# Where low halves lie in memory, and three other edits, in a fused two-block transformer kernel

## The chip, the cores and the metric

The kernel runs on one core of a Trainium2 chip. The metric is the device time of one execution in microseconds (us). Three runs before the change took 733.15 to 735.66, median 735.49.

## The reference

One sequence of 256 tokens, width 1024, passes two blocks. All inputs and outputs are fp32.

```
mod = silu(c) @ w_ada + b_ada                  # six rows: sh1 sc1 g1 sh2 sc2 g2
h = rms(x) * (1 + sc1) + sh1
z = h @ w_in                                   # q, k, v of three mixers, 3072 gate columns
merged = sum over 3 mixers of sigmoid(zg) * (attention @ w_branch)
x = x + g1 * rms(merged @ w_out)
h = rms(x) * (1 + sc2) + sh2
a, g = split(h @ w_up)
x = x + g2 * rms((gelu(conv3(a)) * g) @ w_down)
# second block, two layers
y = gated_linear_attention(x)                  # q, k, v, g, decay; out projection
x = layer_norm(1.414 * x + y)
y = dilated_window_attention(x)                # 3 groups, 8 heads, shared k and v
x = layer_norm(1.414 * x + y)
```

## The kernel before

Every large product is done in three passes of TensorE's fp32r type: a matrix is split into a high half (`hi`, the value rounded to fp32r) and a low half (`lo`, the rest), and `mm3` (L267) adds lo x hi, hi x lo and hi x hi in PSUM. Matmuls are recorded on L262, or on L193 where a `Queue` records them.

Weights come from `Stream` (L105): chunks of 128x2048 land in three `raw` buffers through SP's queue, ScalarE makes `whi` (L158) and VectorE `wlo` (L159), six buffers each. Two forms use them. In `wstat` the weights are the stationary operand and 256 columns of activations move past (chunks `in1`, `inc`, `zg`, `br`, `up`, `gla`, `gk`, `kvk`, `sq`). In `tokmm` 128 activations stand and 512 columns of weights move (`out`, `dn`, `gvg`, `gout`, `kvv`, `sout`).

`PAST` is 48 elements, 192 bytes: each `wlo`, and the low half of the activations (`hlo`, `mlo`, `h2lo`, `flo`, `x2lo`, `olo`, `x3lo`, `slo`, `ylo`), starts 192 bytes into its tile, while the high halves start at the tile's first byte.

PSUM has eight banks: four `acc`, two `mm`, two `at`, each pair or set a ring. The order of instructions on each engine is made by a scheduler from data dependencies and priorities; each engine then runs its list in order.

The places of the change:

- **Modulation.** Beside the mixer's weights, 16 chunks of `w_ada2` are streamed; each costs VectorE two passes into `adacc` (L443, L445). `SIDE` says behind which weight chunk each is fetched: first `inc`, then `zg` 0 to 9, `out` 0 and four `up`.
- **The mixer.** Three attentions are spread between the gate chunks. Each makes `Pat` (softmax, L673 to L680: row maximum on VectorE, exponential and scaling on ScalarE), TensorE transposes it (L688, L696), and then multiplies by v.
- **Gated linear attention (GLA).** `gla_x` makes, per head, the decay exponents on TensorE (`at<-glamr`, four of 128x512), ScalarE takes `E` = exp (L1024), VectorE makes `Xk` and `Xq`. `gla_p` then multiplies these per level (64, 32, ..., 1) into an `at` bank, and VectorE copies the masked part to `attT` (L1044). It runs between the value projection's matmuls.
- **The first layer norm.** `layer_norm` runs by the list `ORD3`: `u` = 1.414x + y with its row sum, `c` = mean, and a Square with row sum on ScalarE, `w` = (u - mean) * g, `r` = (var + eps) to the power -0.5 (GpSimd, L364), `n`/`N` the scaling on ScalarE or VectorE. Eight transposes (L891) for each 128 tokens follow, and then matmuls on `x3`.

Of the kernel before, what the change touches and what calls it, by code (L numbers as in the profile page):

```python
# [14 lines left out]
OP = mybir.AluOpType  # L15
# [9 lines left out]
ALPHA = float(np.float32(4.0 ** 0.25))  # L25
RAWB, HLB, LOOK, LASTF = 3, 6, 2, 4

SIDE = [("inc", 0)] + [("zg", i) for i in range(10)] + [("out", 0)] + [("up", i) for i in (3, 7, 11, 15)]
ORD1 = "s00 m01 s01 m00 r0 a00 S00 a01 S01 m10 s10 R0 A00 A01 s11 r1 m11 n00 n01 a10 S10 a11 S11 A10 R1 A11 N10 n11"
ORD2 = "s00 m01 s01 m00 r0 a00 a01 s10 m10 s11 r1 m11 a10 a11"  # L30
ORD3 = "u00 u01 c0 w00 w01 r0 n00 n01 u10 u11 c1 w10 w11 r1 N10 N11"
ORD4 = "u00 u01 c0 w00 w01 r0 u10 o00 u11 c1 o01 w10 r1 w11 o10 o11"
SC_SWA = float(128.0 ** -0.5)


PAST = 48

COLS = {}
# [64 lines left out]
class Stream:  # L103
# [31 lines left out]
    def _chunk(self, i):  # L135
        nc = self.nc
        key, ap, n, part = self.items[i]
        if part < 0:
            raw = self.early.tile([128, n], F32, tag="early", name="early", bufs=3)
        else:  # L140
            raw = self._raw()
        if not part:
            for o in range(0, n, 1024):
                nc.sync.dma_start(raw[:, o:o + 1024], ap[:, o:o + 1024])
            self.done.append(raw)
            return
        nc.sync.dma_start(raw[:, :n], ap)
        parts = []
        for o in range(0, n, part) if part > 0 else range(0, -part, 1024):
            m = min(part, n - o) if part > 0 else min(1024, -part - o)  # L150
            hi = self.pool.tile([128, 1024], F32R, tag="whi", name="whi", bufs=self.hlbufs)
            lo = self.pool.tile([128, 1088], F32R, tag="wlo", name="wlo", bufs=self.hlbufs)
            lo = lo[:, PAST:PAST + 1024]
            with ExitStack() as st:
                for ins in self.behind:
                    st.enter_context(self.tc.issue_after(ins))
                st.enter_context(self.tc.high_priority(self.pri))
                i0 = nc.scalar.activation(hi[:, :m], raw[:, o:o + m], AF.Copy)  # L158
# [72 lines left out]
def hybrid_blocks(ctx, tc, A, out, dbg=None):  # L231
# [22 lines left out]
    def at_t():  # L254
        return ps.tile([128, 512], F32, tag="at", name="at", bufs=2)
# [100 lines left out]
    def junk():  # L356
        return cn.tile([128, D], BF, name="junk", tag="junk")
# [37 lines left out]
            mm(pr[:, 256 + b:257 + b], ssq[:, b * 128:(b + 1) * 128], ones[:, 0:1], h == 0 and b == 0, h == 3, True)  # L395

    def big8(dt, name, past=0):
        t = cn.tile([128, KK * S + 64 * (past > 0)], dt, name=name, tag="big8l" if past else "big8h")
        return t[:, past:past + KK * S].rearrange("p (k s) -> p k s", k=KK)

    hT = (big8(F32R, "hhi"), big8(F32R, "hlo", PAST))
# [375 lines left out]
    for i in range(2):  # L777
# [12 lines left out]
            branch2(0)  # L790
            branch2(1)
        gates(9 + 2 * i)
    mT = (big8(F32R, "mhi"), big8(F32R, "mlo", PAST))
    for i in range(4):
        if i > 1:
            branch2(i)
# [138 lines left out]
    def ffn_up(f):  # L935
        p = wpair(("up", f), h2, f == 0)
        u = wk.tile([128, S], F32, name="u", tag="u", bufs=2)
        cw = lambda i: col("cw", i * NF + f)
        act.activation(u, p[:, 0:S], AF.Identity, scale=cw(2), bias=col("cb", f))
        dve.scalar_tensor_tensor(u[:, 1:S], p[:, 0:S - 1], cw(1), u[:, 1:S], op0=OP.mult, op1=OP.add)  # L940
        dve.scalar_tensor_tensor(u[:, 2:S], p[:, 0:S - 2], cw(0), u[:, 2:S], op0=OP.mult, op1=OP.add)
        act.activation(u, u, AF.Gelu_apprx_tanh)
        a = wk.tile([128, S], F32, name="fa", tag="fa", bufs=2)
        dve.tensor_mul(a, u, p[:, S:2 * S])
        hi = wk.tile([128, 1, S], F32R, name="fhi", tag="fhi", bufs=6)
        lo = wk.tile([128, 1, S + 64], F32R, name="flo", tag="flo", bufs=6)[:, :, PAST:PAST + S]
# [17 lines left out]
    x2 = res.tile([128, 2, D], F32, name="x2")  # L964
    rms_residual(y2, x1, mod[3], x2, ORD2)
    dump("x2", x2)
    x2T = (big8(F32R, "x2hi"), big8(F32R, "x2lo", PAST))
    ws.behind = transposes(x2, ev_split(x2T), last_mm)


# [41 lines left out]
    def gla_x(b, u):  # L1012
# [3 lines left out]
        XK[b, u] = (Xk, Xq)  # L1016
        nk, nq = (4, 4) if u == 0 else (3, 3) if b == 0 else (3, 4)
        for h in range(4):
            pm = at_t()
            r = glam[:, 4 * u * (1 + b):4 * u * (1 + b) + 4, :]  # L1020
            mm(pm, Ll[:, b, h * 128:(h + 1) * 128], r, True, False)
            mm(pm, Lh[:, b, h * 128:(h + 1) * 128], r, False, True)
            E = p3.tile([128, 4, 128], F32, name="E", tag="E", bufs=2)
            act.activation(E, pm, AF.Exp, scale=1.0 / 16.0)  # L1024
            bs = slice(b * 128, (b + 1) * 128)
            bc = lambda x, n: x[:, h, bs][:, None, :].to_broadcast([128, n, 128])
            dve.tensor_mul(Xk[:, h, 0:nk, :], E[:, 0:nk, :], bc(kT, nk))
            dve.tensor_mul(Xq[:, h, 0:nq, :], E[:, 0:nq, :], bc(qT, nq))
            if u and b == 0:
                dve.tensor_mul(keep[:, h, :], E[:, 3, :], kT[:, h, bs])  # L1030
            if h % 2:
                yield

    def gla_p(b, u):

        Xk, Xq = XK[b, u]
        for l in range(4):
            pp = at_t()
            if 4 * u + l < 7:
                n = 64 >> (4 * u + l)  # L1040
                late = lambda x: x.rearrange("p (g t s) -> p g t s", t=2, s=n)[:, :, 1, :]
                for h in range(4):
                    mm(pp[:, h * 64:(h + 1) * 64].rearrange("p (g s) -> p g s", s=n), Xk[:, h, l, :], late(Xq[:, h, l, :]), True, True)
                dve.copy_predicated(attT[:, 2 * b].rearrange("p h (g t s) -> p h g t s", t=2, s=n)[:, :, :, 1, :],  # L1044
                                    late(glamask[:, 4 * u + l, :])[:, None].to_broadcast([128, 4, 64 // n, n]),
                                    pp[:, 0:256].rearrange("p (h g s) -> p h g s", h=4, s=n))
                continue
            for h in range(4):
                mm(pp[:, h * 128:(h + 1) * 128], kT[:, h, b * 128:(b + 1) * 128], qT[:, h, b * 128:(b + 1) * 128], True, True)
            dve.copy_predicated(attT[:, 2 * b], glamask[:, 4 * u + l, :][:, None, :].to_broadcast([128, 4, 128]),  # L1050
                                pp.rearrange("p (h q) -> p h q", h=4))
        if u and b:
            pp = at_t()
            for h in range(4):
# [103 lines left out]
    def layer_norm(x, y, grow, brow, dst, utile, order, after=None):  # L1158


        qa, qd = Queue(tc, act, ws.last[0]), Queue(tc, dve, ws.last[1])
        su, r, u, w = {}, {}, {}, {}
        with tc.high_priority(BOOST):
            for step in order.split():
                op, b, h = step[0], int(step[1]), int(step[2:] or 0)
                c = half(h)
                if op == "u":
                    if not h:
                        su[b] = cn.tile([128, 6], F32, name="su", tag="su", bufs=2)
                        u[b], w[b] = utile(b), utile(b + 2)  # L1170
                    qd.scalar_tensor_tensor(u[b][:, c], x[:, b, c], ALPHA, y[b][h], op0=OP.mult, op1=OP.add, accum_out=su[b][:, h:h + 1])
                elif op == "c":
                    qd.tensor_scalar(su[b][:, 2:3], su[b][:, 0:1], su[b][:, 1:2], -1.0 / (32.0 * D), op0=OP.add, op1=OP.mult)
                    qd.tensor_scalar(su[b][:, 3:4], su[b][:, 2:3], -32.0, None, op0=OP.mult)
                    qa.activation(junk(), u[b], AF.Square, bias=su[b][:, 2:3], scale=1.0 / 32.0, accum_out=su[b][:, 4:5])
                elif op == "w":
                    qd.scalar_tensor_tensor(w[b][:, c], u[b][:, c], su[b][:, 3:4], grow[:, c], op0=OP.subtract, op1=OP.mult)
                elif op == "r":
                    r[b] = rstd(su[b][:, 4:5], 1, 1e-5, qd)
                elif op == "n":  # L1180
                    qa.activation(dst[:, b, c], w[b][:, c], AF.Copy, scale=r[b][:, 0:1])
                elif op == "N":
# [106 lines left out]
    def swa_pv(i, parts=(slice(0, S),)):  # L1289
# [156 lines left out]
```

## Time and profile before

| | |
|---|---|
| median of three runs | 735.49 us |
| time of the profiled execution | 735.57 us |
| its span, first to last instruction | 733.6 us |
| TensorE matmuls busy | 703.0 us, 96% |
| VectorE busy | 546.9 us, 75% |
| ScalarE busy | 406.9 us, 55% |
| mean granted TensorE clock | 0.987 of full speed |

Matmuls overlap in the records: a 128x256 one is recorded with some 280 ns, while such matmuls start about 116 ns apart. So the pace of a stretch is read from starts, or from a row of the chain, which gives the time and the count of a run of matmuls. 2.0 us of the profiled execution's time lie outside its span.

### The profile page before, as it was taken

How to read it: one execution, taken by the hardware profiler on the slowest of the kernel's cores; microseconds unless marked ns; L12 is line 12 of the kernel's file. 1: busy time of each engine (PE TensorE's matmuls, PEld its weight loads, DVE VectorE, ACT ScalarE, POOL GpSimd, SP SyncE). 2: the span in 40 equal slices, each digit the busy share in tenths (PEclk: the TensorE clock that was granted, in tenths of full speed). 3: DMA queues.
4: the chain of work that ended last, by engine and by line, in shares of the span. 5: the costliest groups of instructions: out<-in, count | busy, mean ns of one | idle time of the engine just before them, and what ended most of it. 6: DMA issues, size and time to landing. Idle time of an engine off the chain costs nothing. (4 is left out here: it accounts for less than half of the span.)

```text
span 733.6 us, 12191 instructions
## 1 busy us (share of the span) xinstructions
PE 703.0 (96%) x4878; PEld 637.2 (87%) x4878; DVE 546.9 (75%) x933; ACT 406.9 (55%) x675; POOL 20.1 (3%) x34
## 2 busy tenths in 40 slices
PE   5999999999989999999999899999989999999995
PEld 4888888998869999998999797888879999999984
DVE  5877969898967776768666766675778689777866
ACT  4447788546547545554544685344546566565542
POOL 0001000000010000000000200001000000000000
PEclk9999999999998999999999999999999999999998
DMA  8996767567744675658645364331347755433201
GB/s 322 422 354 222 281 258 292 207 245 261 242 164 171 236 259 197 230 193 309 245 172 202 125 240 174 116 115 58 144 186 248 255 195 193 156 132 136 96 1 57
DMA packets 24600, 148.74 MB, mean 203 GB/s; under 512 B 2992, under 2 KB 3248, under 8 KB 9568
## 3 DMA queue, kind: packets, MB, share of 16 engines
q1 hardware_dynamic: 21888, 139.05, 51.8%
q0 software_dynamic: 1280, 5.18, 2.2%
q10 hardware_dynamic: 1376, 3.74, 1.5%
q8 instruction: 38, 0.62, 0.3%
q14 instruction: 18, 0.15, 0.1%
HBM read 145.86 MB, written 2.10 MB: 202 GB/s over the span
## 5 line engine op out<-in xcount | busy, mean ns | idle before, releaser
L159 DVE TENSOR_TENSOR wlo<-raw,whi 128x1024 fp32r<-128x1024 f32 (+1 forms) x193 | 231.3, 1210 | 65.6 <-ACT whi L158 65.1
L158 ACT ACTIVATE whi<-raw 128x1024 fp32r<-128x1024 f32 (+1 forms) x193 | 199.3, 1050 | 97.2 <-PE acc L262 42.6
L262 PE MATMUL mm<-h2hi,wlo 128*128 128x256 f32 x352 | 98.6, 281 | 0.0
L262 PE MATMUL mm<-h2hi,whi 128*128 128x256 f32 x352 | 98.5, 281 | 0.0
L262 PE MATMUL mm<-h2lo,whi 128*128 128x256 f32 x352 | 97.3, 283 | 0.0
L262 PE MATMUL mm<-x3hi,wlo 128*128 128x256 f32 x304 | 85.6, 283 | 0.0
L262 PE MATMUL mm<-x3hi,whi 128*128 128x256 f32 x304 | 84.6, 280 | 0.0
L262 PE MATMUL mm<-x3lo,whi 128*128 128x256 f32 x304 | 83.4, 282 | 0.0
L262 PEld LDWEIGHTS mm<-h2hi,wlo 128*128 128x128 f32 x352 | 67.2, 191 | 0.4
L262 PEld LDWEIGHTS mm<-h2hi,whi 128*128 128x128 f32 x352 | 67.2, 191 | 0.0
L262 PEld LDWEIGHTS mm<-h2lo,whi 128*128 128x128 f32 x352 | 65.4, 189 | 0.4
L262 PE MATMUL mm<-hhi,wlo 128*128 128x256 f32 x208 | 60.0, 289 | 0.7 <-DVE wlo L159 0.4
L262 PE MATMUL mm<-hlo,whi 128*128 128x256 f32 x208 | 59.9, 288 | 0.0
L262 PE MATMUL mm<-hhi,whi 128*128 128x256 f32 x208 | 59.3, 285 | 0.0
L262 PEld LDWEIGHTS mm<-x3hi,wlo 128*128 128x128 f32 x304 | 57.6, 190 | 0.0
L262 PEld LDWEIGHTS mm<-x3hi,whi 128*128 128x128 f32 x304 | 57.5, 189 | 0.0
L262 PEld LDWEIGHTS mm<-x3lo,whi 128*128 128x128 f32 x304 | 56.1, 188 | 0.0
L262 PEld LDWEIGHTS mm<-hhi,wlo 128*128 128x128 f32 x208 | 39.8, 191 | 2.8 <-PE mm L262 1.0
L262 PEld LDWEIGHTS mm<-hlo,whi 128*128 128x128 f32 x208 | 39.8, 191 | 0.8 <-issue 0.8
L262 PEld LDWEIGHTS mm<-hhi,whi 128*128 128x128 f32 x208 | 39.7, 191 | 0.6 <-issue 0.5
L445 DVE SCALAR_TENSOR_TENSOR adacc<-raw,cact,adacc 128x1024 f32<-128x1024 f32 x28 | 35.7, 1275 | 0.2
L262 PE MATMUL acc<-whi,flo 128*128 128x512 f32 x88 | 34.9, 397 | 0.0
(355 smaller groups left out, 1608.4 us busy)
## 6 DMA issues: line engine op xcount, KB each, us to landing
raw<-in_w_up_dram SPq DMA_DIRECT2D x22, 1024.0 KB, 4.7
raw<-in_w_ada_dram SPq DMA_DIRECT2D x16, 1024.0 KB, 4.9
raw<-in_swa_q_dram SPq DMA_DIRECT2D x16, 1024.0 KB, 5.2
raw<-in_w_zg_dram SPq DMA_DIRECT2D x12, 1024.0 KB, 5.6
raw<-in_w_dn_dram SPq DMA_DIRECT2D x11, 1024.0 KB, 4.8
raw<-in_w_ada_dram SPq DMA_DIRECT2D x16, 512.0 KB, 9.0
early<-in_w_in_dram SPq DMA_DIRECT2D x8, 1024.0 KB, 7.7
raw<-in_gla_vg_dram SPq DMA_DIRECT2D x8, 1024.0 KB, 4.9
```

What stands on the lines that cost most here:

```text
L158: i0 = nc.scalar.activation(hi[:, :m], raw[:, o:o + m], AF.Copy)
L159: i1 = nc.vector.tensor_sub(lo[:, :m], raw[:, o:o + m], hi[:, :m].bitcast(F32))
L262: return pe.matmul(o, l, r, start=start, stop=stop, skip_group_check=share)
L445: dve.scalar_tensor_tensor(a, w, c, a, op0=OP.mult, op1=OP.add)
```

## The change

1. `wlo` starts 192 bytes in only for chunks whose weights stand (`STILL`); moving `wlo`, and the low halves `mlo`, `flo`, `x2lo`, `olo`, `slo`, lose their shift. `hlo`, `h2lo`, `x3lo` and `ylo` keep it. High and low halves of the large activations now come from one ring of two equal buffers.
2. `SIDE` has no `inc`: the first eleven `w_ada2` chunks are each fetched one weight chunk later.
3. In GLA the exponents alternate between `at` and `mm` banks, and the score levels are laid two to a bank; all levels are multiplied before the copies.
4. The first layer norm takes mean and variance with `bn_stats` and `bn_aggr` on VectorE; the last keeps its sums (steps `U` and `q`). The list of steps is changed with it. The tile of statistics is 16 elements instead of 6.

```diff
-SIDE = [("inc", 0)] + [("zg", i) for i in range(10)] + [("out", 0)] + [("up", i) for i in (3, 7, 11, 15)]
+SIDE = [("zg", i) for i in range(11)] + [("out", 0)] + [("up", i) for i in (3, 7, 11, 15)]
-ORD3 = "u00 u01 c0 w00 w01 r0 n00 n01 u10 u11 c1 w10 w11 r1 N10 N11"
-ORD4 = "u00 u01 c0 w00 w01 r0 u10 o00 u11 c1 o01 w10 r1 w11 o10 o11"
+ORD3 = "u00 v00 u01 v01 c0 r0 w00 w01 n00 n01 u10 v10 u11 v11 c1 r1 w10 n10 w11 N11"
+ORD4 = "U00 U01 q0 w00 w01 r0 U10 o00 U11 q1 o01 w10 r1 w11 o10 o11"
+STILL = ("in1", "inc", "zg", "br", "up", "gla", "gk", "kvk", "sq")
...
-            lo = lo[:, PAST:PAST + 1024]
+            lo = lo[:, PAST:PAST + 1024] if key[0] in STILL else lo[:, 0:1024]
...
-        t = cn.tile([128, KK * S + 64 * (past > 0)], dt, name=name, tag="big8l" if past else "big8h")
+        t = cn.tile([128, KK * S + 64], dt, name=name, tag="big8r", bufs=2)
...
-    mT = (big8(F32R, "mhi"), big8(F32R, "mlo", PAST))
+    mT = (big8(F32R, "mhi"), big8(F32R, "mlo"))
...
-            pm = at_t()
+            pm = mm_t() if h % 2 else at_t()
...
+        levels = [l for l in range(4) if 4 * u + l < 7]
+        banks = [mm_t() if i else at_t() for i in range(2)]
+        for l in levels:
+            n = 64 >> (4 * u + l)
             for h in range(4):
...
+                o = banks[l // 2][:, l % 2 * 256 + h * 64:l % 2 * 256 + (h + 1) * 64]
+                mm(o.rearrange("p (g s) -> p g s", s=n), Xk[:, h, l, :], late(Xq[:, h, l, :], n), True, True)
...
+                        st[b] = cn.tile([128, 16], F32, name="lns", tag="lns", bufs=2)
...
+                elif op == "v":
+                    qd.bn_stats(st[b][:, 6 * h:6 * h + 6], u[b][:, c])
                 elif op == "c":
...
+                    qd.bn_aggr(st[b][:, 12:14], st[b][:, 0:12])
```

**TensorE's list at the start of the GLA scores.** `glamr` are the decay masks, `Ll` and `Lh` the log decays, `x2` the value projection. Before, two heads, four other matmuls, and two heads more in the same two banks:

```order
L262 MATMUL acc<-whi,x2hi 128x512
L262 MATMUL at<-glamr,Ll 128x512
L262 MATMUL at<-glamr,Lh 128x512
L262 MATMUL at<-glamr,Ll 128x512
L262 MATMUL at<-glamr,Lh 128x512
L262 MATMUL acc<-whi,x2lo 128x512
L262 MATMUL acc<-wlo,x2hi 128x512
L262 MATMUL acc<-whi,x2hi 128x512
L262 MATMUL acc<-whi,x2lo 128x512
L262 MATMUL at<-glamr,Ll 128x512
L262 MATMUL at<-glamr,Lh 128x512
```

Now, at the same place (all line numbers are two higher):

```order
L264 MATMUL acc<-whi,x2hi 128x512
L264 MATMUL at<-glamr,Ll 128x512
L264 MATMUL at<-glamr,Lh 128x512
L264 MATMUL mm<-glamr,Ll 128x512
L264 MATMUL mm<-glamr,Lh 128x512
L264 MATMUL at<-glamr,Ll 128x512
L264 MATMUL at<-glamr,Lh 128x512
L264 MATMUL mm<-glamr,Ll 128x512
L264 MATMUL mm<-glamr,Lh 128x512
L264 MATMUL acc<-whi,x2lo 128x512
```

All four heads stand together, in four banks.

**VectorE's list for the second 128 tokens of the first layer norm.** `lnu` is u, `lnw` is w, `su` and `lns` the statistics, `ms` and `rs` the variance and its root. Before:

```order
L193 SCALAR_TENSOR_TENSOR lnu,su<-x_4397,acc 128x512 x2
L193 TENSOR_SCALAR su<-su 128x1 x2
L193 SCALAR_TENSOR_TENSOR lnw<-lnu,su,r_lng_5525 128x512 x2
L193 TENSOR_SCALAR ms<-su 128x1
L193 TENSOR_SCALAR x_5522<-lnw,rs 128x512 x2
```

Now:

```order
L195 SCALAR_TENSOR_TENSOR lnu<-x_4397,acc 128x512
L195 BN_STATS lns<-lnu 128x6
L195 SCALAR_TENSOR_TENSOR lnu<-x_4397,acc 128x512
L195 BN_STATS lns<-lnu 128x6
L195 BN_AGGR lns<-lns 128x2
L195 TENSOR_SCALAR ms<-lns 128x1
L195 SCALAR_TENSOR_TENSOR lnw<-lnu,lns,r_lng_5519 128x512 x2
L195 TENSOR_SCALAR x_5516<-lnw,rs 128x512
```

`ms` stands ahead of both `lnw`, and one of the two last scalings has gone to ScalarE.

**TensorE's list in the mixer, where the first `Pat` is transposed** (`hhi` and `hlo` with a `zg` chunk). Before, from the 465th row of TensorE's list:

```order
L262 MATMUL mm<-hhi,wlo 128x256
L688 MATMUL at<-ident,Pat 128x128
L596 MATMUL at<-ident,vwT 128x128
L688 MATMUL at<-ident,Pat 128x128
L596 MATMUL at<-ident,vwT 128x128
L262 MATMUL mm<-hlo,whi 128x256
```

Now, from the 444th:

```order
L264 MATMUL mm<-hhi,wlo 128x256
L690 MATMUL at<-ident,Pat 128x128
L598 MATMUL at<-ident,vwT 128x128 x2
L690 MATMUL at<-ident,Pat 128x128
L264 MATMUL mm<-hlo,whi 128x256
```

The transposes stand 21 matmuls earlier. The log decay's matmuls (`at<-lf,tri`) that follow stand 32 earlier, and the last `Pat` transposes of the mixer (a block of eight now) some 40 earlier.

## Rows read from the trace of the kernel before

**Rows 1.** The page: span, and busy time of each engine.

```profile
span 733.6 us, 12191 instructions
PE 703.0 (96%) x4878; PEld 637.2 (87%) x4878; DVE 546.9 (75%) x933; ACT 406.9 (55%) x675; POOL 20.1 (3%) x34
```

**Rows 2.** TensorE's waits: us in total, times, longest.

```profile
PE acc L891 <- DVE x L193: 4.1, 3, 2.7
...
PE at L696 <- ACT Pat L680: 1.4, 1, 1.4
PE at L688 <- ACT Pat L680: 1.3, 1, 1.3
PE at L262 <- ACT E L1024: 1.2, 1, 1.2
...
PE at L262 <- DVE attT L1044: 0.3, 1, 0.3
```

**Rows 3.** The chain at the GLA scores: start, us, what.

```profile
449.91 0.60 ACT E L1024
...
450.56 1.23 PE at L262 x4
```

**Rows 4.** Timeline of the first layer norm's end: start, us, engine.

```profile
538.59 1.34 ACT L193 ACTIVATE x<-lnw,rs 128x512 f32<-128x512 f32 x2 [1.09 <-POOL rs L364]
...
540.83 0.69 DVE L193 SCALAR_TENSOR_TENSOR lnu<-x,acc 128x512 f32<-128x512 f32 x1 [2.07 <-PE acc L262]
...
542.00 1.41 DVE L193 SCALAR_TENSOR_TENSOR lnw<-lnu,su,r_lng 128x512 f32<-128x512 f32 x2
...
543.55 0.55 POOL L364 TENSOR_TENSOR rs<-ms,mhalf 128x1 f32<-128x1 f32 x1 [4.99 <-DVE ms L193]
544.14 0.88 DVE L193 TENSOR_SCALAR x<-lnw,rs 128x512 f32<-128x512 f32 x2 [0.67 <-POOL rs L364]
...
544.68 1.97 PE L891 MATMUL acc<-ident,x 128*128 128x128 f32 x8 [2.67 <-DVE x L193]
```

**Rows 5.** Windows at two block ends: length, busy by engine, granted clock, DMA.

```profile
409.00:413.00 4.00, 2.59 (x17) 1.71 (x15) 2.23 (x4) 0.90 (x3) 0.54 (x1) 1.00 0.00 0
...
544.60:546.70 2.10, 2.02 (x10) 2.02 (x11) 0.84 (x4) 1.29 (x4) 0.00 (x0) 0.50 0.69 232
546.70:548.00 1.30, 1.30 (x9) 1.30 (x9) 1.30 (x5) 1.30 (x5) 0.00 (x0) 0.66 0.37 154
```

**Rows 6.** The chain: steady runs of matmuls, 256 wide, 512 wide, and `at<-glamr`.

```profile
466.56 0.92 PE at L262 x4
...
599.06 5.57 PE mm L262 x48
...
635.27 5.57 PE acc L262 x24
```

**Rows 7.** Timeline of TensorE: 512 wide with shift, then attention times v, 512 and 256.

```profile
533.01 0.39 PE L262 MATMUL acc<-whi,olo 128*128 128x512 f32 x1
...
533.23 0.39 PE L262 MATMUL acc<-wlo,ohi 128*128 128x512 f32 x1
...
624.68 0.40 PE L262 MATMUL at<-pTh,svl 128*128 128x512 f32 x1
...
626.07 0.28 PE L262 MATMUL at<-pTh,svl 128*128 128x256 f32 x1
...
627.38 0.28 PE L262 MATMUL at<-pTh,svh 128*128 128x256 f32 x1
```

**Rows 8.** Timeline of VectorE and ScalarE at the mixer's two long waits.

```profile
85.28 1.28 DVE L445 SCALAR_TENSOR_TENSOR adacc<-raw,cact,adacc 128x1024 f32<-128x1024 f32 x1
...
165.52 0.15 DVE L675 TENSOR_SCALAR st<-st 128x4 f32<-128x4 f32 x1
165.58 2.01 ACT L158 ACTIVATE whi<-raw 128x1024 fp32r<-128x1024 f32 x2 [1.32 <-DMA raw<-in_w_br_dram]
...
167.50 0.49 ACT L677 ACTIVATE Pat<-Pat,st 128x256 f32<-128x256 f32 x1
```

More of the change, by code (lines that the diff above doesn't have):

```diff
@@ L945, in ffn_up @@
         hi = wk.tile([128, 1, S], F32R, name="fhi", tag="fhi", bufs=6)
-        lo = wk.tile([128, 1, S + 64], F32R, name="flo", tag="flo", bufs=6)[:, :, PAST:PAST + S]
+        lo = wk.tile([128, 1, S], F32R, name="flo", tag="flo", bufs=6)
         ins = act.activation(hi[:, 0, :], a, AF.Copy)
@@ L966, in hybrid_blocks @@
     dump("x2", x2)
-    x2T = (big8(F32R, "x2hi"), big8(F32R, "x2lo", PAST))
+    x2T = (big8(F32R, "x2hi"), big8(F32R, "x2lo"))
     ws.behind = transposes(x2, ev_split(x2T), last_mm)
@@ L1036, in gla_p @@
         Xk, Xq = XK[b, u]
[L1037 to L1047, printed above, removed]
-            for h in range(4):
-                mm(pp[:, h * 128:(h + 1) * 128], kT[:, h, b * 128:(b + 1) * 128], qT[:, h, b * 128:(b + 1) * 128], True, True)
-            dve.copy_predicated(attT[:, 2 * b], glamask[:, 4 * u + l, :][:, None, :].to_broadcast([128, 4, 128]),
-                                pp.rearrange("p (h q) -> p h q", h=4))
+        late = lambda x, n: x.rearrange("p (g t s) -> p g t s", t=2, s=n)[:, :, 1, :]
@@ new lines, in gla_p @@
+        levels = [l for l in range(4) if 4 * u + l < 7]
+        banks = [mm_t() if i else at_t() for i in range(2)]
+        for l in levels:
+            n = 64 >> (4 * u + l)
+            for h in range(4):
+                o = banks[l // 2][:, l % 2 * 256 + h * 64:l % 2 * 256 + (h + 1) * 64]
+                mm(o.rearrange("p (g s) -> p g s", s=n), Xk[:, h, l, :], late(Xq[:, h, l, :], n), True, True)
+        if u:
+            pd = at_t()
+            for h in range(4):
+                mm(pd[:, h * 128:(h + 1) * 128], kT[:, h, b * 128:(b + 1) * 128], qT[:, h, b * 128:(b + 1) * 128], True, True)
@@ new lines, in gla_p @@
+        for l in levels:
+            n = 64 >> (4 * u + l)
+            dve.copy_predicated(attT[:, 2 * b].rearrange("p h (g t s) -> p h g t s", t=2, s=n)[:, :, :, 1, :],
+                                late(glamask[:, 4 * u + l, :], n)[:, None].to_broadcast([128, 4, 64 // n, n]),
+                                banks[l // 2][:, l % 2 * 256:l % 2 * 256 + 256].rearrange("p (h g s) -> p h g s", h=4, s=n))
+        if u:
+            dve.copy_predicated(attT[:, 2 * b], glamask[:, 7, :][:, None, :].to_broadcast([128, 4, 128]),
+                                pd.rearrange("p (h q) -> p h q", h=4))
@@ L1109, in hybrid_blocks @@
     gla_out(0)
-    oT = (p3.tile([128, KK, S], F32R, name="ohi", tag="Xk"),
-          p3.tile([128, KK * S + 64], F32R, name="olo", tag="Xq")[:, PAST:PAST + KK * S].rearrange("p (k s) -> p k s", k=KK))
+    oT = tuple(p3.tile([128, KK, S], F32R, name=n, tag=t) for n, t in (("ohi", "Xk"), ("olo", "Xq")))
     pe = Queue(tc, pe, ws.last[0])
@@ L1161, in layer_norm @@
         qa, qd = Queue(tc, act, ws.last[0]), Queue(tc, dve, ws.last[1])
-        su, r, u, w = {}, {}, {}, {}
+        st, r, u, w = {}, {}, {}, {}
         with tc.high_priority(BOOST):
@@ L1166, in layer_norm @@
                 c = half(h)
-                if op == "u":
+                if op in "uU":
                     if not h:
-                        su[b] = cn.tile([128, 6], F32, name="su", tag="su", bufs=2)
+                        st[b] = cn.tile([128, 16], F32, name="lns", tag="lns", bufs=2)
                         u[b], w[b] = utile(b), utile(b + 2)
-                    qd.scalar_tensor_tensor(u[b][:, c], x[:, b, c], ALPHA, y[b][h], op0=OP.mult, op1=OP.add, accum_out=su[b][:, h:h + 1])
+                    sums = dict(accum_out=st[b][:, h:h + 1]) if op == "U" else {}
+                    qd.scalar_tensor_tensor(u[b][:, c], x[:, b, c], ALPHA, y[b][h], op0=OP.mult, op1=OP.add, **sums)
+                elif op == "q":
+                    qd.tensor_scalar(st[b][:, 2:3], st[b][:, 0:1], st[b][:, 1:2], -1.0 / (32.0 * D), op0=OP.add, op1=OP.mult)
+                    qd.tensor_scalar(st[b][:, 12:13], st[b][:, 2:3], -32.0, None, op0=OP.mult)
+                    qa.activation(junk(), u[b], AF.Square, bias=st[b][:, 2:3], scale=1.0 / 32.0, accum_out=st[b][:, 13:14])
+                elif op == "v":
+                    qd.bn_stats(st[b][:, 6 * h:6 * h + 6], u[b][:, c])
                 elif op == "c":
-                    qd.tensor_scalar(su[b][:, 2:3], su[b][:, 0:1], su[b][:, 1:2], -1.0 / (32.0 * D), op0=OP.add, op1=OP.mult)
-                    qd.tensor_scalar(su[b][:, 3:4], su[b][:, 2:3], -32.0, None, op0=OP.mult)
-                    qa.activation(junk(), u[b], AF.Square, bias=su[b][:, 2:3], scale=1.0 / 32.0, accum_out=su[b][:, 4:5])
+                    qd.bn_aggr(st[b][:, 12:14], st[b][:, 0:12])
                 elif op == "w":
-                    qd.scalar_tensor_tensor(w[b][:, c], u[b][:, c], su[b][:, 3:4], grow[:, c], op0=OP.subtract, op1=OP.mult)
+                    qd.scalar_tensor_tensor(w[b][:, c], u[b][:, c], st[b][:, 12:13], grow[:, c], op0=OP.subtract, op1=OP.mult)
                 elif op == "r":
-                    r[b] = rstd(su[b][:, 4:5], 1, 1e-5, qd)
+                    r[b] = rstd(st[b][:, 13:14], 1, 1e-5, qd)
                 elif op == "n":
@@ L1293, in swa_pv @@
         hi = wk.tile([128, 2, S], F32R, name="shi", tag="shi", bufs=2)
-        lo = wk.tile([128, 2 * S + 64], F32R, name="slo", tag="slo", bufs=2)[:, PAST:PAST + 2 * S].rearrange("p (u s) -> p u s", u=2)
+        lo = wk.tile([128, 2, S], F32R, name="slo", tag="slo", bufs=2)
         for u in range(2):
```

## The prediction

> **What bounds the kernel now.** I read the page first: TensorE is recorded busy for 703.0 of 733.6 us [rows 1], so time comes off only where TensorE works faster or waits less. The list of its waits comes next. The named waits are few [rows 2]: 4.1 us for the transposes ahead of a new block (of which one wait of 2.7 is the first layer norm's), 1.4 and 1.3 for `Pat` in the mixer, 1.2 for `E` in GLA, 0.3 for `attT`. Third, the chain's runs of matmuls give the pace. With weights standing, 48 matmuls of 256 columns take 5.57 us, 116.0 ns each; with weights moving, 24 of 512 columns take 5.57 us, 232.1 ns each [rows 6]. Last I read the timeline at each place that the change touches. The profiled execution took 735.57 us, of which 733.6 are span, and 735.57 is within 0.1 us of the median of the three runs, so a sum made against it stands for the median too.
>
> **GLA score banks.** The wait of 1.2 us arises because heads 2 and 3 need the two `at` banks of heads 0 and 1, and ScalarE frees the first only after taking `E` (0.60, until 450.51) [rows 3]. With four banks in turn, the order shows all four heads in a row with no bank to wait for: the 1.2 us go. What is late next is `Xk` and `Xq`, which still start when the first `E` is there, at 450.51. TensorE resumed at 450.56 after the wait, so without it, at 449.4. Four exponents and 20 value matmuls followed there before the first scores (four of the 24 that now stand behind the heads were done ahead of the wait): 24 x 232.1 ns [rows 6] = 5.6 us, so the scores come at 455.0. Each head costs VectorE two passes, which I put at `u`'s 0.69 each [rows 4]: three heads are ready 4.1 us after `E`, at 454.6, in time, the fourth at 456.0, which the scores of the other three cover in part. The wait of 0.3 us for `attT` [rows 2] was for an `at` bank that a copy held, and goes as well: the levels have their banks before the copies start. Against it, VectorE may not copy the first level until the second, in the same bank, is multiplied; eight small matmuls, hidden by the value matmuls behind them. The last score levels now share the `mm` ring with `gla_out(0)`, whose squares and scaling fall later; VectorE idled before the gating that needs them, so I cost that at nothing, and at 0.5 us if the cover is too short. Gain: 1.5 us, the two waits; bounds 0 (the first moves to `Xk`) and 1.9, with some switches between fp32 and fp32r runs saved.
>
> **First layer norm.** What ends TensorE's idle time is the path of the second 128 tokens. Before: `u` starts at 540.83, the transposes at 544.68, 3.85 us [rows 4], through two sums, a Square on ScalarE, `ms`, 0.55 on GpSimd and half of the two VectorE scalings (0.44). After: `u` 0.69, `bn_stats`, `bn_aggr`, `ms` 0.15, then the longer of GpSimd's root and the first half of `lnw` (0.71 of 1.41), and a ScalarE scaling of 0.67 (half of 1.34), with some 0.1 us of handovers: 2.3 us plus the two new operations. No row shows these. `bn_stats` reads 512 columns: nearest below is the scaling at 0.44, above it two passes as dear as `u`, 1.4. I take 0.6, near the single pass, since it reads one operand as the scaling does. `bn_aggr` reads 12 numbers: 0.15 (such as `ms`) to 0.4; I take 0.2. Sum 3.1, gain 0.7 us; bounds 1.0 gained and 0.2 lost. For the first 128 tokens the same path ends under the matmuls of the second and costs nothing. The ScalarE Square that falls away hid beside `lnw` in any case.
>
> **Alignment.** Five operand sets lose their shift: `out`, `dn`, `gvg`, `gout`, `sout`, with 32, 88, 64, 32 and 32 triples, so 744 matmuls of 512 columns that now start at the same offset within 256 bytes for both operands. The trace of before has such matmuls: `at<-glamr` runs at 0.92 us for four, 230.0 ns [rows 6], and attention times v at 1.39 us for six, 231.7 ns [rows 7], against 232.1 for the shifted ones. The gain is therefore 744 x 2.1 = 1.6 us by the one and 0.3 by the other; I take 0.8. The 72 triples in which `x2` moves past standing weights lose the shift on `x2lo` alone: 144 matmuls which, by attention times v at 256 columns (1.31 us for eleven, 119.1 ns [rows 7], against 116.0), might each cost 3.1 ns, 0.4 us in all; I take 0.1. Net gain 0.7.
>
> What the trace shows is that a 512-column matmul without any shift takes 230.0 to 231.7 ns. The Trainium skill (TensorE: Matmul & The Clock Gate, Back-to-back issue gap) gives N / 2.4 + 2.5 ns for a matmul with nothing in its way, 215.8 ns at 512 columns. If the shift were all that stands between the two, the sum by that page would be an estimate of 744 x 16.3 ns = 12 us gained; the unshifted rows above already speak against it.
>
> **Modulation.** Each `adacc` pass is 1.28 us [rows 8], so until the chunks have caught up VectorE has one pair, 2.55 us, less ahead of it. But the scheduler has used that: the first `Pat` transposes stand 21 matmuls earlier, 21 x 116.0 ns = 2.4 us. TensorE comes 2.4 us sooner and `Pat` is ready about 2.5 us sooner, so the wait of 1.3 stays. At the log decay TensorE comes 32 x 116.0 = 3.7 us sooner, and ScalarE puts the log ahead of four scalings besides. At the last `Pat` it comes some 40 matmuls, 4.6 us, sooner; VectorE's statistics come 2.5 us sooner, and ScalarE, which did two `whi` (2.01 us) between `st` at 165.52 and the first exponential at 167.50 [rows 8], has one of them ahead now. Together these about cancel. The work is only moved, and no PE row waits for `adacc` itself. I cost this at 0, with bounds of 2.7 gained (both waits of [rows 2] go) and 3 lost (TensorE sooner at three places by up to 1 us more than its data). In SP's queue the `zg` chunk is fetched ahead of the modulation's; no PE wait there names a DMA.
>
> **The sum:** 735.6 - 1.5 - 0.7 - 0.7 - 0 = 732.7; I say 732.6 us. What a measurement of this kernel can tell from no change is about 0.5%, 3.7 us.
>
> **Rivals.**
> *The clock follows.* After the layer norm's wait TensorE's granted clock is 0.50 for 2.1 us and 0.66 for 1.3 more, although after the wait at 409 to 413, shorter, it stays 1.00 [rows 5]. That is half of 2.10 plus a third of 1.30, 1.5 us lost to 1.2 GHz. If the shorter wait keeps 2.4 GHz, and one mixer wait of 1.3 shrinks by half, 730.4; with both mixer waits gone 728.4. For it: VectorE has slack early in the mixer. Against it: the wait is still 1.9 us, not near zero.
> *The mixer takes it back.* The earlier places of transposes and log decay outrun their data, 3 us: 735.6, no change. For it: the 40 matmuls at the last `Pat`, more than I can account for by 1 us. Against: ScalarE's order was moved along with it.
> *Slower: offsets count by themselves.* The new statistics tile is 40 bytes larger, two deep, and in the built program every large operand now starts 128 bytes past a multiple of 256. If a matmul's pace hangs on its own start and not on how its two operands lie to each other, all 3,240 matmuls of 256 columns (1,056 for `up`, 912 for `x3`, 912 for `h`, 216 for `x2`, 144 for the branches) may go from 116.0 to the slowest pace of such matmuls, 119.1 [rows 6, 7]: 10 us, less the 2.9 gained, 742.7. It decides from 2.0 ns each (6.6 us). For it: pace does differ with the operands' places. Against: both operands move together, and nothing in the trace shows a pace worse than 3% off.
> *Alignment frees the whole gap.* The closest starts of two 512-column matmuls in the timeline are 0.22 us apart, 533.01 and 533.23 [rows 7], while their mean is 232.1 ns [rows 6]. If all 744 ran at that closest pace, 744 x 12 ns = 9 us would be gained instead of the 0.8 taken: 724.5. The page named above points the same way. Against it: the unshifted rows take 230.0 to 231.7.
>
> **How the numbers follow.** The forecast, 732.6, has a chance of 0.50 (731 to 734.5); the clock or the mixer's waits go, 0.17; the mixer takes it back, 0.18; slower, 0.09; the whole gap, 0.03; the rest, 0.03, lies between. The range takes in the second and the third: 728.5 to 737.5, and leaves the slow rival and the far end of the waits outside. Faster by over 0.5% (below 731.8) are the second and fifth cases and about a quarter of the first, 0.35; slower (above 739.2) the fourth and a little, 0.10; within 0.5%, 0.55.
>
> **What would show it.** GLA right: no wait of TensorE for `E`, four heads' exponents in a row. Layer norm right: from the last `u` to the transposes about 3.1 us, `bn_stats` near 0.6. Alignment right: 24 moving-weight matmuls in 5.5 to 5.57 us; the standing ones still 5.57 for 48. Modulation right: waits for `Pat` still 1 to 2 us at each place. Wrong would be a `bn_stats` over 1.2 us, a new wait at `at<-lf,tri` or at the last `Pat`, or a pace of standing-weight matmuls other than 116.

## The result, and the profile after

The change makes the kernel faster: 729.34 us median of 14 runs (726.62 to 732.07) against 735.58 (731.63 to 737.73), ratio 0.9923 with a 95% interval of 0.9908 to 0.9939, some 5.7 us by the ratio and 6.2 by the medians. The profiled execution took 729.25 us, and its span was 727.1.

The page of the changed kernel, span and busy time, against [rows 1]:

```profile
span 727.1 us, 12193 instructions
PE 694.4 (95%) x4878; PEld 633.5 (87%) x4878; DVE 549.4 (76%) x930; ACT 405.3 (56%) x672; POOL 21.0 (3%) x34
```

Its waits of TensorE (total, times, longest), against [rows 2]:

```profile
PE acc L893 <- ACT x L195: 2.5, 1, 2.5
...
PE at L698 <- ACT Pat L682: 2.1, 2, 1.7
PE at L690 <- ACT Pat L682: 1.8, 2, 1.4
```

The waits for `E` and `attT` are gone; the layer norm's 2.7 is now 2.5; `Pat` holds TensorE up more in total, not less, in four places instead of two. So the named waits do not explain the gain. Where it lies is read from the starts of the first matmul of each stage in both traces:

| stretch, from the first matmul of its kind to the next stage's | before | after | difference |
|---|---|---|---|
| start to the gates (`mm<-hhi,wlo`) | 66.20 | 66.14 | -0.1 |
| the mixer, to the out projection (`acc<-wlo,mhi`) | 125.48 | 123.48 | -2.0 |
| out projection and first residual, to `up` | 30.99 | 30.62 | -0.4 |
| up and down, to the transposes of x | 186.99 | 184.99 | -2.0 |
| from there to the first exponent of GLA | 37.68 | 38.83 | +1.2 |
| GLA scores, to `at<-vg,attT` | 60.17 | 57.59 | -2.6 |
| GLA out, to the first 128 tokens' transposes of the layer norm | 33.11 | 32.73 | -0.4 |
| from there, with the layer norm's wait and `x3` past standing weights, to `x3` with moving ones | 23.30 | 23.37 | +0.1 |
| the rest | 169.64 | 169.38 | -0.3 |

The sum is -6.4; the spans differ by 6.5 as printed. Some of these differences are clock alone: in both traces TensorE is granted 0.50 of full speed (1.2 GHz) after some of the long waits, but not after the same ones. Before, that was so behind the first residual and behind the layer norm, and once in the mixer; after, behind the first residual for a shorter time (1.0 of the 2.0 us of up and down) and behind both later norms (some 0.9 of the +1.2). In the changed kernel it is also so for 10 us before the gates, where it cost nothing (66.14 against 66.20). Windows of the changed kernel at the layer norm, against [rows 5]:

```profile
539.00:542.00 3.00, 3.00 (x16) 2.96 (x15) 2.34 (x6) 3.00 (x9) 0.00 (x0) 0.50 0.92 341
542.00:543.00 1.00, 1.00 (x9) 1.00 (x8) 1.00 (x4) 1.00 (x2) 0.00 (x0) 0.80 1.01 397
```

The slightly shorter wait did not keep 2.4 GHz: 0.50 is 1.2 GHz, for 3 us and a part of the fourth.

The chain of the changed kernel shows the pace, 24 matmuls with moving weights and 48 with standing ones, against [rows 6]:

```profile
629.07 5.47 PE acc L264 x24
...
635.41 5.57 PE mm L264 x48
```

5.47 us for 24 are 227.9 ns each, against 232.1; the standing ones are as before. The timeline at the GLA scores, TensorE's first and last exponent matmul and the first `E` on ScalarE, against [rows 3]:

```profile
444.07 0.39 PE L264 MATMUL at<-glamr,Ll 128*128 128x512 f32 x1
...
445.65 0.39 PE L264 MATMUL mm<-glamr,Lh 128*128 128x512 f32 x1
...
446.64 0.60 ACT L1026 ACTIVATE E<-at 128x512 f32<-128x512 f32 x1
```

All eight exponent matmuls are issued before the first `E` starts, 7 steps in 1.58 us, some 226 ns each. The timeline of the layer norm's second 128 tokens, against [rows 4]:

```profile
534.59 0.69 DVE L195 SCALAR_TENSOR_TENSOR lnu<-x,acc 128x512 f32<-128x512 f32 x1 [0.31 <-PE acc L264]
535.31 0.69 DVE L195 BATCH_NORM_STATS2 lns<-lnu 128x6 f32<-128x512 f32 x1
...
536.03 0.21 DVE L195 BATCH_NORM_AGGREGATE lns<-lns 128x2 f32<-128x12 f32 x1
536.28 0.15 DVE L195 TENSOR_SCALAR ms<-lns 128x1 f32<-128x1 f32 x1
536.35 1.40 DVE L195 SCALAR_TENSOR_TENSOR lnw<-lnu,lns,r_lng 128x512 f32<-128x512 f32 x2
536.51 0.99 POOL L366 TENSOR_TENSOR rs<-ms,mhalf 128x1 f32<-128x1 f32 x1 [3.82 <-DVE ms L195]
537.53 0.72 ACT L195 ACTIVATE x<-lnw,rs 128x512 f32<-128x512 f32 x1 [3.47 <-POOL rs L366]
537.86 0.49 DVE L195 TENSOR_SCALAR x<-lnw,rs 128x512 f32<-128x512 f32 x1
...
538.31 1.36 PE L893 MATMUL acc<-ident,x 128*128 128x128 f32 x8 [2.55 <-ACT x L195]
```

From the last `u` to the transposes it is 3.72 us, against 3.85; I had said 3.1.

### The profile page after: what moved, and what is told of

Its sections match the earlier page's. It is cut to its first block, busy times and chain, and to the rows that moved or that the text cites. A ratio compares the mean times of both kernels' runs of the same rounds, so it can differ in the third digit from the quotient of the medians.

```text
span 727.1 us, 12193 instructions
## 1 busy us (share of the span) xinstructions
PE 694.4 (95%) x4878; PEld 633.5 (87%) x4878; DVE 549.4 (76%) x930; ACT 405.3 (56%) x672; POOL 21.0 (3%) x34
```

## The experiments

**Alignment alone.** The kernel before with edit 1 (lines of the diff on `STILL`, `big8`, `flo`, `oT`, `slo`).

```diff
-            lo = lo[:, PAST:PAST + 1024]
+            lo = lo[:, PAST:PAST + 1024] if key[0] in STILL else lo[:, 0:1024]
```

> The kernel before with edit 1 alone (low halves unshifted where weights move; every large operand still starts at a multiple of 256 bytes), all instruction lists as before. Theory A, what counts is how the two operands lie to each other: the moving-weight matmuls fall to the pace that the whole change shows, acc<-whi,fhi and acc<-whi,flo from a mean of 235 to about 228 ns, and the time falls by 744 x 4.5 ns = 3 us (0.45%). Theory B, the start at 128 past a multiple of 256, which edit 4's larger tile brought, makes the pace: here they stay at 230 to 232 ns and the time falls by 0.3 to 1.5 us.

Measured: 733.63 us against 735.62, ratio 0.9976 (0.9952 to 1.0001). The stages give the finer answer, since no list differs: out projection -0.36 us, up and down -1.0 beside the clock, GLA and its projections -0.7, the last out projection -0.26; against them +0.4 where `x2` moves past standing weights. Net -1.9 us. 24 moving-weight matmuls take 5.47 us:

```profile
630.28 5.47 PE acc L263 x24
```

Theory A holds for the pace, and its 3 us come out as 1.9 net. The timed runs agree but cannot show it by themselves: their interval just reaches 1.

**The start of the tiles.** The whole change with the statistics in the `junk` tile, so that all large operands start at multiples of 256 bytes again.

```diff
-                        st[b] = cn.tile([128, 16], F32, name="lns", tag="lns", bufs=2)
+                            if not b:
+                                lns = cn.tile([128, D // 2], F32, name="lns", tag="junk")
+                            st[b] = lns[:, 16 * b:16 * b + 16]
```

> The whole change with the first layer norm's statistics kept in the junk tile, so that every large operand starts at a multiple of 256 bytes again; TensorE's list is the same to the row. Theory A: paces and time as with the whole change, 0.992 of before. Theory B: the moving-weight matmuls go back from 227 to 230 to 232 ns, some 3 us longer than the whole change, 0.996.

Measured: 729.21 us, ratio 0.9918 (0.9889 to 0.9947). Its chain has the same two paces:

```profile
629.16 5.47 PE acc L264 x24
...
635.50 5.56 PE mm L264 x48
```

A start 128 bytes further for all of them together does nothing; my slower rival falls.

**No shift, and a shift of 64 bytes.** What a shift is worth where weights stand, in the whole change.

```diff
-PAST = 48
+PAST = 0
```

> The whole change with no shift at all (PAST 0: standing wlo, hlo, h2lo, x3lo, ylo start at their tiles' first byte too), every list as in the whole change. Theory A, equal offsets are fast for every form, as they are where weights move: 48 standing-weight matmuls fall from 5.57 us to 5.45 (113.5 ns each), 3,240 of them 8 us in all, 0.982 of before. Theory B, where weights stand the three passes read the moving operand and the next standing one together and equal offsets clash, as the branch decay shows where x2lo lost its shift (mm<-x2lo,whi 119 and mm<-x2hi,whi 121 ns against 118 and 115): 48 take 5.65 to 5.76 us, 5 to 13 us lost, 0.999 to 1.010.

Measured: 740.45 us, ratio 1.0093 (1.0058 to 1.0128), which is 0.017 or some 12 us above the whole change. The chain:

```profile
643.98 5.47 PE acc L264 x24
...
650.33 5.76 PE mm L264 x48
```

Theory B: with equal offsets 48 standing-weight matmuls take 5.76 us, 120.0 ns each, instead of 116.0. The same equality that speeds up the one form slows down the other.

Then with `PASTA` 16 (64 bytes) for `hlo`, `h2lo`, `x3lo` and `ylo`, and 48 as before for the weights:

```diff
-    hT = (big8(F32R, "hhi"), big8(F32R, "hlo", PAST))
+    hT = (big8(F32R, "hhi"), big8(F32R, "hlo", PASTA))
```

> The whole change with the low halves of the standing-weight activations (hlo, h2lo, x3lo, ylo) 64 bytes into their tiles instead of 192; standing wlo stay at 192. Theory A, a matmul's pace is set by how its moving operand lies to the standing operand that is loaded next, and 64 bytes apart costs less (115.4 ns, as mm<-x3hi,whi) than 192 (118.3, as mm<-x3lo,whi): mm<-x3lo,whi and mm<-h2lo,whi fall to 115 to 116 ns, 48 standing-weight matmuls from 5.57 to 5.52 us, the time by up to 1080 x 2.9 ns = 3 us, 0.988 of before. Theory B, 192 and 64 cost alike and the order of the three passes sets it: paces stay, 0.992.

Measured: 735.41 us, ratio 1.0012 (0.9989 to 1.0035). Both theories fall: the paces neither fell nor stayed but rose, to 5.65 us for 48:

```profile
640.88 5.65 PE mm L264 x48
```

So for standing weights a shift of 192 bytes on both low halves is the best of the three tried (116.0 ns), then 64 on the activations' (117.7), then none (120.0). Neither of the rules I had written down gives these numbers; what rule does stays open.

**Score banks alone**, edit 3 on the kernel before.

```diff
-            pm = at_t()
+            pm = mm_t() if h % 2 else at_t()
```

and `gla_p` as in the change.

> The kernel before with edit 3 alone (score banks). Theory A, the waits for E and for attT go and nothing else: GLA from the first exponent matmul to the first of the diagonal value products (at<-vg,attT) 58.6 us instead of 60.2, the time 1.5 us shorter (0.2%). Theory B, the grouping of the scores saves as much again in switches between fp32 and fp32r runs: 57.6 to 58.0 us, 2.2 to 2.6 us shorter (0.3%).

Measured: 733.50 us, ratio 0.9973 (0.9952 to 0.9993); GLA 58.00 us instead of 60.17, 2.2 less. Theory B by its range. Then the line above alone, with the score levels as before:

> The kernel before with the exponents alone on alternating at and mm banks (the score levels as before). Read by the length of GLA, first exponent matmul to first at<-vg,attT: 60.17 us before, 58.00 with the whole of edit 3. Theory A, the two named waits are all there is, and this half takes the one for E: 58.9 us, which leaves 0.9 to the score levels, 0.3 for attT and 0.6 for fewer switches between fp32 and fp32r runs. Theory B, the exponents in a row save the switches too: 58.0 to 58.3 us, and the score levels bring next to nothing.

Measured in one execution: GLA 58.46 us, between the two ranges. So the exponents' banks bring 1.7 us and the score levels 0.5.

**Layer norm alone**, edit 4 on the kernel before, with its statistics in the `junk` tile.

```diff
+                elif op == "v":
+                    qd.bn_stats(st[b][:, 6 * h:6 * h + 6], u[b][:, c])
...
+                    qd.bn_aggr(st[b][:, 12:14], st[b][:, 0:12])
```

> The kernel before with edit 4 alone (first layer norm by bn_stats, its statistics in the junk tile, so that every large operand stays at a multiple of 256 bytes). Theory A, my sum: path from the last u to the transposes 3.1 us, 0.7 us shorter, and the clock may stay at 2.4 GHz for 1.5 more: 0.997 to 0.999. Theory B, by the rows of the whole change (bn_stats 0.69, GpSimd's root 0.99 instead of 0.55 beside lnw): the path is 3.7 us, TensorE waits some 0.1 us less, and the time is the same, 1.000.

Measured: 735.21 us, ratio 1.0004 (0.9979 to 1.0029); the wait ahead of the transposes is 2.5 instead of 2.7. Theory B.

**`u` left in PSUM**, in the whole change, to see what slows GpSimd's root.

```diff
-                    qd.scalar_tensor_tensor(u[b][:, c], x[:, b, c], ALPHA, y[b][h], op0=OP.mult, op1=OP.add, **sums)
+                    ub = (lambda b, h: y[b][h]) if "v" in order else (lambda b, h: u[b][:, half(h)])
+                    qd.scalar_tensor_tensor(ub(b, h), x[:, b, c], ALPHA, y[b][h], op0=OP.mult, op1=OP.add, **sums)
```

> The whole change with u of the first layer norm left in the PSUM banks that y came in, so that lnw reads one operand from SBUF instead of two; no list changes otherwise. Theory A, GpSimd's root takes 0.99 us because lnw's two SBUF operands hold what GpSimd reads through: the root falls to 0.55 beside lnw, and the transposes start 0.4 us sooner after the last u. Theory B, the root is slow for another reason (its own start): it stays at 0.99 and the wait stays at 2.5 us. The whole time moves by under 0.1% either way, so the rows decide.

Measured: 729.18 us, ratio 0.9927 (0.9904 to 0.9951), as the whole change. Its timeline at the same place:

```profile
536.13 0.70 DVE L195 SCALAR_TENSOR_TENSOR acc<-x,acc 128x512 f32<-128x512 f32 x1 [0.28 <-PE acc L264]
...
537.90 1.40 DVE L195 SCALAR_TENSOR_TENSOR lnw<-acc,lns,r_lng 128x512 f32<-128x512 f32 x2
538.06 0.56 POOL L366 TENSOR_TENSOR rs<-ms,mhalf 128x1 f32<-128x1 f32 x1 [4.24 <-DVE ms L195]
538.74 0.72 ACT L195 ACTIVATE x<-lnw,rs 128x512 f32<-128x512 f32 x1 [3.46 <-DVE lnw L195]
...
538.79 0.41 PE L893 MATMUL acc<-ident,x 128*128 128x128 f32 x2 [2.26 <-DVE lnw L195]
539.41 0.49 DVE L195 TENSOR_SCALAR x<-lnw,rs 128x512 f32<-128x512 f32 x1
...
539.51 1.31 PE L893 MATMUL acc<-ident,x 128*128 128x128 f32 x10 [0.31 <-ACT x L195]
```

Theory A on the root: 0.56 beside an `lnw` that reads one operand from SBUF, 0.99 beside one that reads two. From the last `u` to ScalarE's scaling it is 2.61 us, against 2.94 in the changed kernel. But `u` now sits in `acc` banks, the ring that the transposes write: four transposes run, and for the next TensorE waits 2.26 us until `lnw` has read a bank [2.26 <-DVE lnw]. So this run shows what slows the root, and not what a faster root alone would be worth.

**Modulation alone**, edit 2 on the kernel before, and then the whole change without it (the same line turned back):

```diff
-SIDE = [("inc", 0)] + [("zg", i) for i in range(10)] + [("out", 0)] + [("up", i) for i in (3, 7, 11, 15)]
+SIDE = [("zg", i) for i in range(11)] + [("out", 0)] + [("up", i) for i in (3, 7, 11, 15)]
```

> The kernel before with edit 2 alone (SIDE). Theory A, the moved modulation chunks shorten the mixer as the whole change shows: from the first gate matmul (mm<-hhi,wlo) to the first of the out projection 123.5 us instead of 125.5, and the time falls by about 2 us (0.3%). Theory B, my forecast that earlier places and later data cancel, and the whole change's mixer was short for some other reason: 125 to 126 us and the same time.

Measured: 734.75 us, ratio 0.9983 (0.9965 to 1.0002), mixer 124.46 us. Between the theories.

> The whole change with the SIDE table of before (edit 2 undone). Theory A, edit 2 earns the mixer's 2 us of the whole change: the time comes back to 0.9945 to 0.996 of before, and the mixer (first mm<-hhi,wlo to first acc<-wlo,mhi) to 125 us. Theory B, the mixer's length swings from run to run with stretches of the 1.2 GHz clock and edit 2 is worth nothing: 0.992, as the whole change.

Measured: 731.12 us, ratio 0.9950 (0.9925 to 0.9976), mixer 126.95, longer than Theory A's 125. By its ratio 0.0027, 2.0 us, slower than the whole change: Theory A's time, though the two intervals overlap by a little. Six profiled executions have the old table and, in the mixer, the same lists on TensorE; four have the new one (the two with other offsets for standing weights come behind the table):

| kernel | table | longest wait for the first `Pat` | ScalarE waits for `raw` in the mixer | mixer, us | its mean granted clock |
|---|---|---|---|---|---|
| before | old | 1.3 | 14.3 | 125.48 | 0.99 |
| alignment alone | old | 1.2 | 10.1 | 122.97 | 1.00 |
| exponent banks alone | old | 1.2 | 12.1 | 123.68 | 1.00 |
| score banks alone | old | 2.9 | 12.4 | 128.53 | 0.97 |
| change without edit 2 | old | 2.8 | 12.3 | 126.95 | 0.99 |
| layer norm alone | old | 2.7 | 12.4 | 128.47 | 0.97 |
| the change | new | 1.4 | 6.7 | 123.48 | 1.00 |
| the change, base 0 | new | 0.9 | 5.8 | 123.07 | 1.00 |
| modulation alone | new | 1.5 | 6.4 | 124.46 | 0.99 |
| `u` in PSUM | new | 1.2 | 4.3 | 124.22 | 0.99 |

With the old table the same lists have a mixer of 123.0 to 128.5 us, mean 126.0; with the new one 123.1 to 124.5, mean 123.8. Best against best they are equal. The two with the new table and other offsets are longer: 126.43 with 64 bytes, with a wait of 0.4 for the first `Pat`, and 128.49 without a shift, with a wait of 2.5; their standing-weight matmuls are slower as well, so their lengths cannot be set beside the others'. What goes with the long mixers of the old table is a wait of ScalarE and one of VectorE for DMA ahead of the first `Pat`. Here they are in the layer norm's run (old table), with the window around them:

```profile
87.37 1.28 DVE L445 SCALAR_TENSOR_TENSOR adacc<-raw,cact,adacc 128x1024 f32<-128x1024 f32 x1 [1.26 <-DMA raw<-in_w_ada_dram]
...
89.70 0.17 DVE L678 RECIPROCAL st<-st 128x4 f32<-128x4 f32 x1
...
89.87 1.06 ACT L158 ACTIVATE whi<-raw 128x1024 fp32r<-128x1024 f32 x1 [1.29 <-DMA raw<-in_w_zg_dram]
90.83 1.26 ACT L680 ACTIVATE Pat<-Pat,st 128x128 f32<-128x128 f32 x4
```

```profile
84.00:96.00 12.00, 8.26 (x56) 7.80 (x55) 10.34 (x29) 9.79 (x29) 0.00 (x0) 0.86 0.66 241
```

and in the changed kernel, the scaling and the window:

```profile
86.02 1.26 ACT L682 ACTIVATE Pat<-Pat,st 128x128 f32<-128x128 f32 x4
```

```profile
84.00:96.00 12.00, 10.59 (x91) 10.22 (x90) 10.01 (x24) 11.57 (x33) 0.00 (x0) 1.00 0.77 286
```

ScalarE's list has a `whi` ahead of `Pat`'s scaling. With the old table its `zg` chunk stands behind one more modulation chunk in SP's queue and lands late in some executions; ScalarE then waits 1.3 to 1.5 us with the scaling behind it, TensorE waits 2.7 to 2.9 instead of 1.2 to 1.3. In the same three executions, and in none of the other three, VectorE waits 1.3 to 1.5 us for a modulation chunk, ahead of the reciprocal that the scaling needs. In the rows above the scaling starts when `whi` is done, 0.96 us after the reciprocal, so ScalarE's chunk held it up last; but with ScalarE in time the scaling would still have waited for VectorE. No run separates the two chunks. In two of the three such runs the granted clock falls behind it (0.86 over the 12 us, so 0.14 x 12 = 1.7 us lost).

The new table does not rule this out. In the run without a shift, which has it, the chunk is late at the same place, and TensorE waits 2.5 for the first `Pat`:

```profile
88.43 1.06 ACT L160 ACTIVATE whi<-raw 128x1024 fp32r<-128x1024 f32 x1 [1.72 <-DMA raw<-in_w_zg_dram]
```

**One chunk later still**, and **one chunk fetched twice**, both in the whole change.

```diff
-SIDE = [("zg", i) for i in range(11)] + [("out", 0)] + [("up", i) for i in (3, 7, 11, 15)]
+SIDE = [("zg", i) for i in range(1, 12)] + [("out", 0)] + [("up", i) for i in (3, 7, 11, 15)]
```

> The whole change with the modulation chunks one weight chunk later still (behind zg 1 to 11 and out 0). Theory A, the mixer is held up by weights that land late behind modulation chunks in SP's queue at its start, and each chunk taken from there helps: ScalarE's waits for raw in the mixer fall below the 5.3 us (after) and the time to 0.989 to 0.991 of before. Theory B, one chunk was enough: the mixer stays at 122.5 to 123.5 us outside slow-clock stretches and the time at 0.992; the last sums, which come later, may cost 0.5 us at the first residual.

Measured: 731.62 us, ratio 0.9957 (0.9940 to 0.9975), slower than the change. Both theories fall; ScalarE's waits for `raw` in the mixer rose to 16.0 us, where Theory A had them fall. Its first `Pat` stands 12 rows earlier again, and TensorE outruns it, as my second rival had it for the change: the wait is 2.5 and the granted clock falls behind it (mixer 125.98).

```profile
PE at L690 <- ACT Pat L682: 3.5, 2, 2.5
```

```diff
+            if i < 18:
+                self.nc.sync.dma_start(raw, ap)
             self.side = self.nc.sync.dma_start(raw, ap).ins
```

> The whole change with the first modulation chunk fetched twice into the same buffer: 1 MB more in SP's queue ahead of the second zg chunk, with no more work on VectorE (the scheduler puts the first Pat and the log decay some 20 rows later for it). Theory A, what edit 2 removes is lateness of weights: ScalarE waits for raw again (over 10 us in the mixer, as with the old table), the mixer takes 124.5 to 126 us without slow-clock stretches and the time goes to 0.994 to 0.996. Theory B, what it removes is VectorE's pair of sums ahead of Pat: the mixer stays at 122.5 to 123.5 us and the time at 0.992.

Measured: 730.41 us, ratio 0.9946 (0.9922 to 0.9970), mixer 125.23. The time is Theory A's, its two marks are not: ScalarE waits 6.1 us for `raw`, not over 10, and less the 1.7 us of clock the mixer is 123.5. The scheduler had moved `Pat` and the log decay, so the run does not separate lateness from order; what it has in common with two of the three long mixers is a wait of 2.5 or more for the first `Pat` and a clock that falls behind it, here with neither DMA wait just ahead of the scaling.

```profile
84.00:96.00 12.00, 9.55 (x69) 9.25 (x69) 11.36 (x23) 11.85 (x35) 0.00 (x0) 0.86 0.83 298
```

No version that was tried is faster than the change by more than the noise.

## Why the prediction was right, and short by half

The time lies in the range, the sign is right, and the mechanisms of edits 1 and 3 are. The size was 2.9 where some 6 were measured. That the range held is in part luck: 729.3 lies outside the 731 to 734.5 of the forecast's own case, in the part that the range took in for the rival that the clock follows, and that rival's mechanism, a wait behind the layer norm short enough to keep 2.4 GHz, did not happen. Term by term:

*GLA score banks, 1.5 forecast, 2.2 measured.* The waits went as described, and `Xk` was in time; the gain lies above the upper bound of 1.9. The extra is split between the halves: the banks of the exponents brought 1.7, 0.5 more than the wait for `E`, the score levels 0.5, 0.2 more than the wait for `attT`. That fewer switches between fp32 and fp32r runs make up these 0.7 us fits, but was not tried by itself.

*Alignment, 0.7 forecast, 1.9 net measured.* I took 1.1 ns for each of the 744 matmuls, between two rows of before that I held to be without shift [rows 6, 7]. They were no measure: the same exponent matmuls, 230.0 ns there, take some 226 in the changed kernel, and four of them 0.91 us (227.5 each) with alignment alone, so it is not their grouping. 24 matmuls in a run save 4.2 ns each, twice the upper bound of 2.1. On the other side the 72 triples of `x2` cost 0.4 us where I took 0.1; there the bound was right, and the choice between the bounds was not. The rival of the whole gap, 12 ns each, falls: 227.9 ns is where equal offsets end, not 220.

By the Trainium skill's formula (TensorE: Matmul & The Clock Gate, Back-to-back issue gap) the estimate for this is 215.8 ns; no run of such matmuls here at a granted clock of 1.00 came to it as a pace.

*Layer norm, 0.7 forecast, 0.1 measured.* `bn_stats` took 0.69 (0.6 forecast) and `bn_aggr` 0.21 (0.2). The step that failed is "then the longer of GpSimd's root and the first half of `lnw` (0.71 of 1.41), and a ScalarE scaling of 0.67". The root ran beside `lnw` and took 0.99, not the 0.55 that it takes alone [rows 4], and so it, not the half `lnw`, set when ScalarE's scaling could start. Of the 0.6 us by which the path missed 3.1, the root is 0.28 (0.99 for 0.71), `bn_stats` 0.09, the scaling 0.05 (0.72 for 0.67), and the handovers some 0.2. Nor was the root all: the other half is scaled by VectorE behind both `lnw`, and VectorE's own list, 0.69 + 0.69 + 0.21 + 0.15 + 1.40 + 0.49 = 3.6 us, ends at 538.35, as late as ScalarE's scaling at 538.25. The transposes were released by ScalarE's; what a faster root would bring is not shown, since the run with `u` in PSUM put a wait for banks in its place.

That the root is held up by a VectorE instruction with two SBUF operands is also what the Trainium skill says (SBUF — State Buffer, Who interferes with whom: only the port pair shared by VectorE and GpSimd contends, as an exclusive lock); the rows agree, 0.99 with two such operands, 0.56 with one.

The rival that the clock follows did not come about here, and its price was too high. One execution, that of the change without edit 2, kept a granted clock of 1.00 behind the same wait of 2.5 us:

```profile
542.00:545.00 3.00, 3.00 (x21) 2.45 (x19) 1.90 (x5) 2.77 (x8) 0.00 (x0) 1.00 0.90 309
```

Its stretch from the first transposes to `x3` with moving weights took 22.95 us, against 23.37 in the changed kernel with the same lists there: the slow clock costs some 0.4 us there, not the 1.5 that the rival took. Why this one execution kept its clock stays open.

*Modulation, 0 forecast, 0.9 to 2.0 measured.* The step that failed is "The work is only moved [...] I cost this at 0", and behind it "no PE wait there names a DMA". I read the wait of 1.3 from one execution; it was one of the good ones. The same lists give 2.7 to 2.9 in others, since ScalarE and VectorE, not TensorE, wait for the DMA, and the scaling of `Pat` stands behind both. Between two good executions my cancelling is borne out: best against best, the two mixers are equal to 0.1 us (122.97 and 123.07). What the edit seems to bring is that late chunks come together with `Pat` less often: in three of six executions with the old table, in none of the four with the new one, and again in the one without a shift. That is argued from a few executions, not shown. By the timed runs the edit is worth 0.9 us alone and 2.0 within the change, and neither figure is clear of noise: the first interval reaches 1.0002, the second overlaps that of the change. Why some of these mixers have a granted clock below 1 between 131 and 139 us and others don't stays open.

1.9 + 2.2 + 0.1 and 0.9 to 2.0 make 5.1 to 6.2 us, where 5.7 to 6.2 were measured. The ratios of the four edits alone multiply to 0.9936, 4.7 us.

## What to carry to other kernels

A wait read from one profiled execution is one draw: where it ends in an engine that itself converts DMA'd data, ask what the lists of that engine and of those that feed it have ahead of the releasing instruction, and look at a second execution before a cost is put at nothing. An operation that will run beside another engine's work is not to be priced by a row in which it ran alone. Where a path runs over one engine, add up that engine's whole list to the last instruction that the waiting engine needs, not only to the first. An operand's offset has to be tried for each form of matmul: the same 192 bytes that help one cost the other.

## What the runs showed of the hardware that I had not expected

The pace of an fp32r matmul depends on how far apart its operands and their low halves start, in opposite ways for the two forms here: with 512 columns of weights moving 227.9 ns at equal offsets and 232.1 with the low halves 192 bytes further; with 256 columns moving past standing weights 120.0 at equal offsets, 116.0 at 192, 117.7 with the activations' half at 64 and the weights' at 192. Moving everything by 128 bytes changes nothing. The two forms differ in width as well as in which operand moves; no run separates these.

A longer wait can cost twice: of the six executions in which TensorE waited 2.5 to 2.9 us for the first `Pat`, five went on at 1.2 GHz for a while, 1.7 us more by the granted clock; of the eight with 0.4 to 1.5 us, none did at that place. Between the longest mixer and the one whose clock did not fall there (128.53 and 126.95, waits of 2.9 and 2.8) lie 1.6 us. What the slow clock costs hangs on the place: 0.4 us behind the layer norm.
